# A weighted sum of two experts' outputs: the first tile loaded in one DMA in place of two

## The chip, the cores and the metric

The kernel runs on one core of a Trainium2 chip. The metric is the device time of one execution in microseconds (us), as the median of several runs. The profile is one execution taken by the hardware profiler; its span is a little shorter than the time (237.3 us against 239.03), since it starts with the first instruction.

The engines that matter here are VectorE (called DVE in the profile), ScalarE (ACT), SyncE (SP), and the core's 16 DMA engines, which move data between the chip's main memory (HBM) and the on-chip memory of 128 partitions. DMAs are issued by SyncE and by ScalarE. Each of the two has a DMA queue of its own: q1 is SyncE's, q10 is ScalarE's.

## The reference

For each of 16 x 1024 = 16,384 tokens there are two vectors of 512 floats, one from each of two experts, and two weights. The result is their weighted sum.

```python
def setup_inputs():
    batch, seq, hidden, n_experts, k = 16, 1024, 512, 8, 2
    return {
        "expert_outputs": np.random.randn(batch, seq, k, hidden).astype(np.float32),
        "combine_weights": np.random.randn(batch, seq, k).astype(np.float32),
    }

def reference(expert_outputs, combine_weights):
    weights = combine_weights[..., np.newaxis]
    return np.sum(expert_outputs * weights, axis=2).astype(np.float32)
```

The kernel must read 67.1 MB of vectors and 0.13 MB of weights and write 33.6 MB. There are two products and one addition for every element of the result.

## The kernel before

A token is a row of 1024 floats (4 KB): the 512 of the first expert, then the 512 of the second. Each of the 128 partitions has 128 tokens: 120 in ten tiles of 12 (`J`, g = 0 to 9), and 8 (`LAST`) in a last tile, g = 10. In memory the 120 tokens of one partition lie side by side, so a tile of 12 tokens is one contiguous run of 48 KB in each partition. There are four tile buffers (`bufs=4`).

```python
    J, LAST = 12, 8
    main = per - LAST                      # 120
    ...
    last = main // J                       # 10
    wpool = ctx.enter_context(tc.tile_pool(name="w", bufs=1))
    ipool = ctx.enter_context(tc.tile_pool(name="in", bufs=4))
    wt = wpool.tile([P, per * k], dt)

    for t, c in ((0, main), (main, LAST)):      # weights: rows of 960 B, then of 64 B
        nc.scalar.dma_start(
            out=wt[:, k * t : k * (t + c)].rearrange("p (t k) -> p t k", k=k), in_=cw(t, c)
        )
    ...
    for g in range(last + 1):
        et = ipool.tile([P, J, k * h], dt)
        ot = ...                                # the result, in the front half of et itself
        t0, c = g * J, J if g < last else LAST

        for a, m in ((0, 2), (2, c - 2)) if g == 0 else ((0, c),):
            nc.sync.dma_start(
                out=et[:, a : a + m],
                in_=eo(t0 + a, m),
                max_dma_last_dim=k * h * 4 if g + a == 0 else None,
            )
        if g < last - 1:                        # tiles 0 to 8
            wb = wt[:, g * J * k : (g + 1) * J * k].unsqueeze(2).to_broadcast([P, J * k, h])
            ek = et.rearrange("p j (k h) -> p (j k) h", k=k)
            nc.vector.tensor_tensor(out=ek, in0=ek, in1=wb, op=mult)
            nc.vector.tensor_tensor(out=ot, in0=et[:, :, 0:h], in1=et[:, :, h : 2 * h], op=add)
            nc.scalar.dma_start(out=o(t0, c), in_=ot)
            continue
        ...                                     # tiles 9 and 10: ScalarE takes the first product,
                                                # VectorE the rest
        nc.sync.dma_start(out=o(t0, c), in_=ot[:, 0:c])
```

The weights are loaded in two DMAs from ScalarE's queue: 120 tokens' weights (960 B in each partition) and those of the last tile (64 B). Tile 0 is loaded in two DMAs: tokens 0 and 1, cut into rows of 4 KB by `max_dma_last_dim`, and tokens 2 to 11 in rows of 40 KB. All other tiles of 12 come in one DMA with rows of 48 KB. The first VectorE product of a tile covers all of its 12 tokens and is one instruction. A buffer is loaded anew when its result has been stored.

Of the kernel before, what the change touches and what calls it, by code (L numbers as in the profile page):

```python
# [1 line left out]

# [4 lines left out]


@with_exitstack
def kernel(  # L10
    ctx: ExitStack,
    tc: tile.TileContext,
    expert_outputs: bass.AP,
    combine_weights: bass.AP,
    out: bass.AP,
):

    nc = tc.nc  # L20
    b, s, k, h = expert_outputs.shape
    assert k == 2
    n = b * s
    P = nc.NUM_PARTITIONS
    per = n // P
    assert per * P == n
    J, LAST = 12, 8
    main = per - LAST
    assert main % J == 0
    eo = expert_outputs.rearrange("b s k h -> (b s) (k h)")  # L30
    cw = combine_weights.rearrange("b s k -> (b s) k")
    o = out.rearrange("b s h -> (b s) h")

    def rows(x):

        a = x[0 : P * main, :].rearrange("(p t) f -> p t f", p=P)
        b = x[P * main : n, :].rearrange("(p t) f -> p t f", p=P)
        return lambda t, c: a[:, t : t + c, :] if t < main else b[:, t - main : t - main + c, :]

    eo, cw, o = rows(eo), rows(cw), rows(o)  # L40

    dt = mybir.dt.float32
    mult = mybir.AluOpType.mult
    add = mybir.AluOpType.add
    copy = mybir.ActivationFunctionType.Copy

    last = main // J
# [6 lines that stand above are left out]
    for t, c in ((0, main), (main, LAST)):  # L54
        nc.scalar.dma_start(
            out=wt[:, k * t : k * (t + c)].rearrange("p (t k) -> p t k", k=k), in_=cw(t, c)
        )

    warm = wpool.tile([P, 1], dt)
    nc.scalar.activation(out=warm, in_=nc.const_aps.tensor(1.0, (P, 1), dt), func=copy)  # L60

    for g in range(last + 1):
        et = ipool.tile([P, J, k * h], dt)

        ot = et.rearrange("p j f -> p (j f)")[:, 0 : J * h].rearrange("p (j f) -> p j f", f=h)
        t0, c = g * J, J if g < last else LAST

        for a, m in ((0, 2), (2, c - 2)) if g == 0 else ((0, c),):
            nc.sync.dma_start(  # L69
                out=et[:, a : a + m],  # L70
                in_=eo(t0 + a, m),
                max_dma_last_dim=k * h * 4 if g + a == 0 else None,
            )
        if g < last - 1:

            wb = wt[:, g * J * k : (g + 1) * J * k].unsqueeze(2).to_broadcast([P, J * k, h])
# [7 lines that stand above are left out]
        for i in range(c):  # L84
            t = t0 + i
            nc.scalar.activation(  # L86
                out=et[:, i, 0:h], in_=et[:, i, 0:h], func=copy, scale=wt[:, 2 * t : 2 * t + 1]
            )
            if g == last:
                nc.vector.scalar_tensor_tensor(  # L90
                    out=ot[:, i, :],
                    in0=et[:, i, h : 2 * h],
                    scalar=wt[:, 2 * t + 1 : 2 * t + 2],
                    in1=et[:, i, 0:h],
                    op0=mult,
                    op1=add,
                )
        if g < last:
            w1 = wt.rearrange("p (t k) -> p t k", k=k)[:, t0 : t0 + c, 1:2]
            x1 = et[:, :, h : 2 * h]  # L100
            nc.vector.tensor_tensor(out=x1, in0=x1, in1=w1.to_broadcast([P, c, h]), op=mult)  # L101
            nc.vector.tensor_tensor(out=ot, in0=et[:, :, 0:h], in1=x1, op=add)  # L102
        nc.sync.dma_start(out=o(t0, c), in_=ot[:, 0:c])


# [1 line left out]
_INS = ['expert_outputs', 'combine_weights']  # L107
_OUTS = [((16, 1024, 512), 'float32')]


# [23 lines left out]
```

## Time and profile before

| | before |
|---|---|
| time, median of 3 runs | 239.03 us (238.98 to 239.05) |
| span of the profile | 237.3 us |
| VectorE busy | 193.9 us (82%) |
| ScalarE busy | 14.0 us (6%) |
| moved by DMA | 100.80 MB, 425 GB/s over the span |
| VectorE product of 12 tokens (line L78), mean | 12.96 us |
| VectorE sum of 12 tokens (line L79), mean | 6.56 us |
| a load of 12 tokens, 6144 KB, median from issue to landing | 29.9 us |
| a store of 12 tokens, 3072 KB, median from issue to landing | 32.7 us |

How to read it: the DMA row of the page cuts the span into 40 slices and gives the busy share of the 16 DMA engines in tenths. A line of a DMA queue gives packets, MB, and the time that the packets took as a share of 16 engines' span. A packet here is one contiguous row, or a completion signal of 4 bytes, of which each DMA leaves one on each of the 16 engines. The chain of waits is followed back from the last instruction, at each step to what released it. A line of DMA issues gives the size of one DMA and the time from its issue to the landing of its last byte; that time includes waiting behind other transfers. In a line of the timeline the bracket tells how long the engine stood idle before the instruction, and for what. In a line of the windows stand busy time and number of instructions of DVE, ACT and POOL, the clock of TensorE (not used here), the share of time of the 16 DMA engines by packets that start in the window, and GB/s.

### The profile page before, as it was taken

To read this page: it belongs to the slowest core of one execution; us is meant where nothing else is said; L and a number is where in the kernel's file an instruction comes from. 1 tells how busy PE (TensorE), PEld (TensorE's weight loads), DVE (VectorE), ACT (ScalarE), POOL (GpSimd) and SP (SyncE) were. 2 spreads that over 40 slices of the span, in tenths; PEclk is the share of its full clock that TensorE was granted. 3 is DMA by queue.
4 is the path that set the end of the run, shared out by engine and by line. 5 is a ranking of instruction groups with operands and counts; after the bars stand their busy time and mean duration, and the time that the engine had idled before them with its cause. 6 is when DMAs were issued, how large, how long until landed. Compare 5 with 4: busy or idle time off the path is not lost.

```text
span 237.3 us, 154 instructions
## 1 busy us (share of the span) xinstructions
DVE 193.9 (82%) x28; ACT 14.0 (6%) x22; POOL 0.2 (0%) x4
## 2 busy tenths in 40 slices
DVE  0008999999999999999999879969996998785710
ACT  2000000000000000000000000000000000740800
POOL 0000000000000000000000000000000000000000
DMA  8999999989899999999897999999997979999997
GB/s 308 443 456 406 398 431 497 398 356 505 356 439 435 427 464 464 398 398 522 348 522 344 452 427 435 464 464 398 398 522 340 530 336 460 458 403 442 402 438 309
DMA packets 3728, 100.80 MB, mean 425 GB/s; under 512 B 528, under 2 KB 656, under 8 KB 912
## 3 DMA queue, kind: packets, MB, share of 16 engines
q1 hardware_dynamic: 2144, 72.35, 71.1%
q10 hardware_dynamic: 1584, 28.44, 27.9%
HBM read 67.24 MB, written 33.55 MB: 425 GB/s over the span
## 4 chain that ended last, share of the span: by engine, by line
DMA 59%; DVE 33%; ACT 2%; DVEq 0%; ACTq 0%; issue 0%; SPq 0%
DMA et<-in_expert_outputs_dram 30%; DMA out_dram<-et 29%; DVE et L78 22%; DVE et L79 11%; ACT et L86 2%; DVE et L90 1%; DVEq L129 0%; ACTq L129 0%; SPq L69 0%; DVEq L78 0%; ACTq L86 0%
## 5 line engine op out<-in xcount | busy, mean ns | idle before, releaser
L78 DVE TENSOR_TENSOR et<-et,wt 128x12288 f32<-128x12288 f32 x9 | 116.6, 12955 | 25.2 <-DMA et<-in_expert_outputs_dram 25.2
L79 DVE TENSOR_TENSOR et<-et 128x6144 f32<-128x6144 f32 x9 | 59.0, 6558 | 0.3
L86 ACT ACTIVATE et<-et,wt 128x512 f32<-128x512 f32 x20 | 12.5, 707 | 209.2 <-DMA et<-in_expert_outputs_dram 209.2
L90 DVE SCALAR_TENSOR_TENSOR et<-et,wt 128x512 f32<-128x512 f32 x8 | 5.6, 748 | 3.9 <-ACT et L86 3.7
L101 DVE TENSOR_TENSOR et<-et,wt 128x6144 f32<-128x6144 f32 x1 | 6.6, 6559 | 2.3 <-DMA et<-in_expert_outputs_dram 2.3
L102 DVE TENSOR_TENSOR et<-et 128x6144 f32<-128x6144 f32 x1 | 6.6, 6559 | 0.9 <-ACT et L86 0.9
L60 ACT ACT_TABLE_LOAD x1 | 1.3, 1283 | 1.7 <-issue 1.7
L60 ACT ACTIVATE warm<-const-float32-1.0 128x1 f32<-128x1 f32 x1 | 0.2, 202 | 0.0
L118 POOL MEMSET const-bfloat16-1.0<- 128x1 bf16 x1 | 0.1, 102 | 0.0
L118 POOL MEMSET const-uint8-127<- 128x1 uint8 x1 | 0.1, 102 | 0.0
L118 POOL MEMSET const-float32-0.0<- 128x1 f32 x1 | 0.1, 99 | 0.2 <-issue 0.2
L118 POOL MEMSET const-float32-1.0<- 128x1 f32 x1 | 0.1, 99 | 0.0
## 6 DMA issues: line engine op xcount, KB each, us to landing
et<-in_expert_outputs_dram SPq DMA_DIRECT2D x9, 6144.0 KB, 29.9
out_dram<-et ACTq DMA_DIRECT2D x9, 3072.0 KB, 32.7
et<-in_expert_outputs_dram SPq DMA_DIRECT2D x1, 5120.0 KB, 17.3
et<-in_expert_outputs_dram SPq DMA_DIRECT2D x1, 4096.0 KB, 25.1
out_dram<-et SPq DMA_DIRECT2D x1, 3072.0 KB, 14.6
out_dram<-et SPq DMA_DIRECT2D x1, 2048.0 KB, 10.0
et<-in_expert_outputs_dram SPq DMA_DIRECT2D x1, 1024.0 KB, 5.4
wt<-in_combine_weights_dram ACTq DMA_DIRECT2D x1, 120.0 KB, 4.4
```

The costliest lines, as they stand in the source:

```text
L60: nc.scalar.activation(out=warm, in_=nc.const_aps.tensor(1.0, (P, 1), dt), func=copy)
L78: nc.vector.tensor_tensor(out=ek, in0=ek, in1=wb, op=mult)
L79: nc.vector.tensor_tensor(out=ot, in0=et[:, :, 0:h], in1=et[:, :, h : 2 * h], op=add)
L86: nc.scalar.activation(out=et[:, i, 0:h], in_=et[:, i, 0:h], func=copy, scale=wt[:, 2 * t : 2 * t + 1])
L90: nc.vector.scalar_tensor_tensor(out=ot[:, i, :], in0=et[:, i, h : 2 * h], scalar=wt[:, 2 * t + 1 : 2 * t + 2], in1=et[:, i, 0:h], op0=mul ...
L101: nc.vector.tensor_tensor(out=x1, in0=x1, in1=w1.to_broadcast([P, c, h]), op=mult)
L102: nc.vector.tensor_tensor(out=ot, in0=et[:, :, 0:h], in1=x1, op=add)
L118: nc = _bacc.Bacc("TRN2", target_bir_lowering=False, num_devices=1)
```

## The change

Tile 0 is loaded like all the others: one DMA of 12 tokens in rows of 48 KB. The two DMAs of before, with 256 rows of 4 KB and 128 rows of 40 KB, become one with 128 rows of 48 KB. The purpose is a simpler start, with fewer DMAs and only long rows.

```diff
-        for a, m in ((0, 2), (2, c - 2)) if g == 0 else ((0, c),):
-            nc.sync.dma_start(
-                out=et[:, a : a + m],
-                in_=eo(t0 + a, m),
-                max_dma_last_dim=k * h * 4 if g + a == 0 else None,
-            )
+        nc.sync.dma_start(out=et[:, 0:c], in_=eo(t0, c))
```

## The prediction

> **What bounds the kernel now.** I read the page from the top: busy time of each engine, the DMA row over the span, the DMA queues, then the chain of waits.
>
> ```profile
> span 237.3 us, 154 instructions
> DVE 193.9 (82%) x28; ACT 14.0 (6%) x22; POOL 0.2 (0%) x4
> DMA  8999999989899999999897999999997979999997
> DMA packets 3728, 100.80 MB, mean 425 GB/s; under 512 B 528, under 2 KB 656, under 8 KB 912
> q1 hardware_dynamic: 2144, 72.35, 71.1%
> q10 hardware_dynamic: 1584, 28.44, 27.9%
> DMA 59%; DVE 33%; ACT 2%; DVEq 0%; ACTq 0%; issue 0%; SPq 0%
> ```
>
> VectorE, the busiest engine, has 18% of the span free; the DMA engines have none. The packets of the two queues took 71.1% + 27.9% = 99.0% of 16 engines' span, 234.9 us for each engine. The trace's records of single packets agree: the first data packet starts at 1.81 us, the last ends at 236.18, and I find no gap in between in which an engine stood still for more than 0.15 us. Of the 237.3 us, 1.8 are the start before data moves, 1.1 the end after the last packet, and 234.4 are 16 engines working without a pause (the records overlap by a few ns, so their sum is a little above). The dips to 7 in the DMA row are slices that long packets straddle: a packet is counted where it starts.
>
> The chain of waits names DVE for 33%, but that is a path through a loop (a load needs a free buffer, which needs a store, which needs DVE). As long as either queue has something to move, a delay on that path costs nothing. Its beginning, which the change touches:
>
> ```profile
> 1.22 17.29 DMA et<-in_expert_outputs_dram
> 18.51 0.03 issue
> 18.54 0.05 DVEq L78
> 18.59 0.05 issue
> 18.64 12.97 DVE et L78
> 31.60 0.02 issue
> 31.63 6.56 DVE et L79
> ```
>
> The chain starts at the second DMA, not the first: DVE's first product waits for both halves of tile 0 and for the main weight load. The 1024 KB half arrives 5.4 us after its issue and lies unused until 18.5.
>
> ```profile
> et<-in_expert_outputs_dram SPq DMA_DIRECT2D x1, 5120.0 KB, 17.3
> et<-in_expert_outputs_dram SPq DMA_DIRECT2D x1, 1024.0 KB, 5.4
> wt<-in_combine_weights_dram ACTq DMA_DIRECT2D x1, 120.0 KB, 4.4
> wt<-in_combine_weights_dram ACTq DMA_DIRECT2D x1, 8.0 KB, 17.1
> ```
>
> Look at the last two: the 8 KB of weights need 17.1 us to land and the 120 KB only 4.4. Both are 128 short rows, 8 on each DMA engine. The difference is what stands in the other queue: 4 KB rows in the first case, 40 KB rows in the second.
>
> **What the Trainium skill says.** "DMA: Bandwidth & Descriptors", section "Queues, rings and completion order", says that each DMA engine goes round-robin between its queues, a whole packet at a time. The trace agrees: behind the short rows each engine's records alternate, one 40960-byte packet (1.514 us), one 64-byte packet (0.011 us), and eight such rounds, 8 x 1.52 = 12.2 us, are the bulk of those 17.1. The same page's section "Issuing engines are not separate DMA queues" says that transfers from different queues share the same 16 engines; so a saturated kernel cannot gain by order alone, and the 99.0% above says this one is saturated. Under "Where 436 GB/s comes from" the page gives a ceiling of 435 GB/s; the mean here is 425, and a long packet's rate is 49152 B / 1.815 us x 16 = 433 GB/s.
>
> **The change part by part.** On every engine the compute instructions and their order stay the same; one DMA issue leaves SyncE. Per DMA engine:
>
> 1. Packets removed: 16 of 4096 B (128 partitions x 2 tokens, 256 in all) at a steady 0.159 us = 2.54 us; 8 of 40960 B at 1.514 = 12.11; one completion packet, 0.01. Together 14.67.
> 2. Packets added: 8 of 49152 B at 1.815 (median of the 1152 there now) = 14.52 us. Saved: 14.67 - 14.52 = **0.15 us**, all of it on the saturated resource.
> 3. The ramp. The 256 short packets took 3.21 us per engine in sum, 0.67 more than 16 x 0.159: the first ones last 0.2 to 1.0 us each. The windows of 1 us show it (the last two numbers are DMA share and GB/s):
>
> ```profile
> 1.00:2.00 1.00, 0.00 (x0) 0.26 (x1) 0.00 (x0) 1.00 0.40 61
> 2.00:3.00 1.00, 0.00 (x0) 1.00 (x1) 0.00 (x0) 1.00 0.77 182
> 3.00:4.00 1.00, 0.00 (x0) 0.22 (x2) 0.00 (x0) 1.00 1.00 371
> 4.00:5.00 1.00, 0.00 (x0) 0.00 (x0) 0.00 (x0) 1.00 1.08 430
> ```
>
> With 48 KB rows some of this excess may vanish, if it is paid per packet, or none, if it belongs to the first moments of reading. I book 0 to 0.4 us saved, middle 0.1.
>
> 4. The weights come later. Now 8 rows of 960 B (0.044 us each) slip between 4 KB rows. After the change each waits for a 48 KB row. In the records of before most engines start with two packets of the load queue, then alternate strictly. Carried over: rows 1 and 2, weight row 1, row 3, weight row 2, and so on to row 8, weight row 7, tile 0's completion, weight row 8, the first row of tile 1, the weights' completion. So I expect the 120 KB to land one long packet, 1.8 us, behind tile 0. Tile 0's data end at about 1.9 (mean first packet) + 14.52 + 7 x 0.044 + a ramp of 0.3 to 0.7 = 17.0 to 17.4 us; some 0.6 us more to landing and 1.8 for the weights puts DVE's first product at 19.5 to 20.2, say **19.9 instead of 18.6**. The 8 KB of weights follow eight or more rounds later, at 35 to 39; only the last tile reads them, past 200 us.
> 5. Does the 1.3 us matter? DVE runs tiles 0 to 5 back to back, 12.95 + 6.56 us each (the pair's period is 19.46), until 135.5 and then waits:
>
> ```profile
> 137.66 12.96 DVE L78 TENSOR_TENSOR et<-et,wt 128x12288 f32<-128x12288 f32 x1 [2.17 <-DMA et<-in_expert_outputs_dram]
> 159.43 12.96 DVE L78 TENSOR_TENSOR et<-et,wt 128x12288 f32<-128x12288 f32 x1 [2.21 <-DMA et<-in_expert_outputs_dram]
> ```
>
> So DVE catches up at tile 6 at the latest. What a late DVE can do earlier is send out the first store late: 39.5 instead of 38.2 us. The store queue then starts about one long packet later, and the load queue gets one packet ahead. The engines stay busy, since the loads of tiles 1 to 3 are queued until 72 us (the longest load lands 69.3 us after issue), and the fifth load, which waits for the first store, is issued at 64.15: 8 us in hand. At the end, the last store is issued at 226.5 and by the packet records the store ahead of it on the same queue moves until 231.2. With the 1.1 us from issue to first packet there are 3.6 us in hand. Neither margin is used up by 1.3 us, or by 1.8.
>
> Sum: -0.15 (packets) - 0.1 (ramp) + 0 (late weights) = -0.25 us, so **238.8 us**.
>
> **The rivals.** *The late weights reach the end.* If the 1.3 to 1.8 us of DVE were on the path all the way, the time would be 240.3 to 240.8, and with two long packets of delay 242.6. For it: the chain's first third is DVE back to back behind that wait. Against: the 99.0%, DVE's waits of 2.2 us at tiles 6 to 8, the margins of 8 and 3.6 us. Even this is at most 1.5%.
>
> *The ramp goes away.* If all 0.67 us of the short rows' excess is due to their being short, the time is 239.03 - 0.15 - 0.67 = 238.2. For it: the excess sits in the first one to three short packets of each engine. Against: at 39 to 42 us, just when the first store is on its way (issued at 38.22), load packets of 48 KB last up to 2.42 us in place of 1.815, a loss of some 0.6 us per engine; the first use of a direction seems to cost as much with long rows.
>
> *The ramp grows.* Long rows could bind an engine longer to a slow first access; 0.3 us more would give 239.2.
>
> **Range and chances.** The three runs of before lie within 0.07 us, and the sum's terms are fractions of a microsecond, so the range holds the ramp either way and a little of a late tail: 238.2 to 239.5. A change of 2% is 4.8 us, more than the rivals make, two of them together included. Faster 0.01, same 0.98, slower 0.01.
>
> **What would show it right or wrong.** Right: q1 has 272 packets less (256 + 128 rows removed, 128 added, 16 completions less: 2144 - 272 = 1872); the two shares still sum to 99%; the 120 KB of weights land at 18 to 20 us after issue, the one 6144 KB load of tile 0 at about 17; DVE starts at 19.5 to 20.2; its wait at tile 6 shrinks from 2.17 us to under 1. If DVE starts at 18 us, step 4 (two load packets before the first weight row) is wrong. If the packets' shares fall below 98%, step 5 is wrong and there is idle DMA time to be found, first about 64 to 72 us or after 226. If the 1 us windows show the ramp reaching 430 GB/s at another time, step 3 is what was mis-sized.

## The result: 0.3% slower at the median, and scattered

The changed kernel takes 239.80 us at the median of 6 runs (239.11, 239.14, 239.72, 239.88, 240.15, 240.50). The kernel before takes 238.99 (238.93 to 239.05). The ratio is 1.0031, with a 95% interval of 1.0016 to 1.0046. That is within the 2% that was forecast as near certain, but outside the forecast range of 238.2 to 239.5, and of the other sign than the forecast gain of 0.25 us. The scatter is the first thing to notice: 0.12 us before, 1.4 us after. A part of the difference is luck. All six runs of the kernel before were quick, but beside the experiments below 27% of its runs (81 of 299) were not; at that share six quick ones in a row are an estimated one case in seven. By the means of the larger sets below, the change costs 0.2 to 0.3 us (239.59 against 239.41, and 239.65 against 239.38).

The page of the changed kernel, from its top, in the profiled run (239.88 us):

```profile
span 238.1 us, 154 instructions
DVE 194.0 (81%) x28; ACT 14.0 (6%) x22; POOL 0.2 (0%) x4
DMA  7999999999999999999999999899999999999995
DMA packets 3456, 100.80 MB, mean 423 GB/s; under 512 B 512, under 2 KB 640, under 8 KB 640
q1 hardware_dynamic: 1872, 72.35, 70.8%
q10 hardware_dynamic: 1584, 28.44, 27.8%
```

The 272 packets fewer on q1 are there. The two shares sum to 98.6% of 238.1 us, 234.8 us for each engine, against 234.9 before. So the DMA engines have no more to do, yet the span is 0.8 us longer. The dips of before are gone from the DMA row: packets no longer start in lockstep on all engines. The last slice fell from 7 to 5.

The lines of the DMA issues and the start of the chain of waits:

```profile
et<-in_expert_outputs_dram SPq DMA_DIRECT2D x10, 6144.0 KB, 31.6
wt<-in_combine_weights_dram ACTq DMA_DIRECT2D x1, 120.0 KB, 17.7
wt<-in_combine_weights_dram ACTq DMA_DIRECT2D x1, 8.0 KB, 31.8
```

```profile
0.72 17.67 DMA wt<-in_combine_weights_dram
18.39 0.02 issue
18.41 12.97 DVE et L73
```

The weights now land last, as foreseen, but at 18.39, hardly behind tile 0. DVE starts at 18.41, 0.23 us earlier than before. A late start of DVE is not the cause. DVE's wait at tile 6 did not shrink to under 1 us either: it is 2.29 us, and a new one of 1.70 us stands at tile 5.

```profile
117.51 12.96 DVE L73 TENSOR_TENSOR et<-et,wt 128x12288 f32<-128x12288 f32 x1 [1.70 <-DMA et<-in_expert_outputs_dram]
139.35 12.96 DVE L73 TENSOR_TENSOR et<-et,wt 128x12288 f32<-128x12288 f32 x1 [2.29 <-DMA et<-in_expert_outputs_dram]
```

The loads come late: a load takes 31.6 us from issue to landing at the median, 1.7 us more than before, almost one 48 KB packet.

### Where the time is: one DMA engine out of sixteen

The windows of 1 us around the first store, and the one at the end, of the changed kernel (DMA share and GB/s are the last two numbers; a window counts the packets that start in it):

```profile
41.00:42.00 1.00, 1.00 (x1) 0.00 (x0) 0.00 (x0) 1.00 1.99 713
42.00:43.00 1.00, 1.00 (x1) 0.00 (x0) 0.00 (x0) 1.00 0.17 49
43.00:44.00 1.00, 1.00 (x1) 0.00 (x0) 0.00 (x0) 1.00 0.98 418
236.00:237.00 1.00, 0.00 (x0) 0.00 (x0) 0.00 (x0) 1.00 0.04 16
```

The same windows of the kernel before:

```profile
41.00:42.00 1.00, 1.00 (x1) 0.00 (x0) 0.00 (x0) 1.00 2.18 737
42.00:43.00 1.00, 1.00 (x1) 0.00 (x0) 0.00 (x0) 1.00 0.00 0
43.00:44.00 1.00, 1.00 (x1) 0.00 (x0) 0.00 (x0) 1.00 0.91 393
236.00:237.00 1.00, 0.00 (x0) 0.00 (x0) 0.00 (x0) 1.00 0.00 0
```

A number of GB/s in a window of 1 us is kilobytes. Before: 393 is 16 x 24.576, so all 16 engines start their first store row in 43 to 44, and none starts anything in 42 to 43. After: 713 is 14 x 49.152 + 24.576, so one engine has begun its first store row before 42, and the 49 in the next window are its next load row alone. And at the end, one 16 KB row of the last store starts after 236.0, by itself; before, none does.

The trace has each DMA packet's start and duration but not its engine. I joined the packets to 16 chains by end and start. For the changed kernel (us; "extra" is the duration above the median of packets of that size):

```
                     first packet  first store row  extra at 36-48 us  end
the engine in question   1.86          41.88             1.26          236.96
the other fifteen     1.75-2.63     43.08-43.80       0.20-0.68     235.67-236.20
kernel before, all 16 1.81-2.10     43.26-43.78       0.60 (mean)   235.72-236.18
```

The engine that takes the store first pays for it: its load packet before the store lasts 2.24 us and the one after 2.65, in place of 1.815. On the other fifteen these two last 1.97 to 2.38 and 1.81 to 2.03 us, so the difference is in the one after. Every DMA is divided evenly over the engines, 8 rows to each: every one of the 16 chains, the late one too, has 80 load rows of 48 KB and 80 store rows of 24 KB. So nobody takes over what one engine has lost; it stays behind to the end, 0.77 us after the next one, and the span ends with it.

### The profile page after: what moved, and what is told of

It is laid out like the page before. It is cut to its first block, busy times and chain, and to the rows that moved or that the text cites. A ratio compares the mean times of both kernels' runs of the same rounds, so it can differ in the third digit from the quotient of the medians.

```text
span 238.1 us, 154 instructions
## 1 busy us (share of the span) xinstructions
DVE 194.0 (81%) x28; ACT 14.0 (6%) x22; POOL 0.2 (0%) x4
## 4 chain that ended last, share of the span: by engine, by line
DMA 60%; DVE 33%; ACT 2%; DVEq 0%; ACTq 0%; issue 0%; SPq 0%
DMA out_dram<-et 28%; DMA et<-in_expert_outputs_dram 25%; DVE et L73 22%; DVE et L74 11%; DMA wt<-in_combine_weights_dram 7%; ACT et L81 2%; DVE et L85 1%; DVEq L124 0%; ACTq L124 0%; SPq L68 0%; DVEq L73 0%; ACTq L81 0%
## 6 DMA issues: line engine op xcount, KB each, us to landing
et<-in_expert_outputs_dram SPq DMA_DIRECT2D x10, 6144.0 KB, 31.6
```

## The experiments

The theory to test (theory 1): the first store reaches the 16 engines close to their packet boundaries. Depending on a tenth of a microsecond, one or more engines take it one 48 KB packet earlier than the rest. Those out of step lose 0.5 to 1 us there, and the slowest engine sets the end. The rivals: the long first rows make the start uneven (theory 2), and late weights or later work of VectorE (theory 3). Runs fall into two groups, 238.9 to 239.4 and 239.5 to 241.3 us, with only 12 of the 641 runs between; I count those at 239.5 and above as the upper group. The groups are clear in the two kernels themselves, less so in some variants. The experiments ran on several chips, each beside many runs of the kernel before.

**a_again** is the changed kernel as it is.

> The changed kernel once more, for the spread of its times and a second profile. Theory 1 (one or a few of the 16 DMA engines take the first store's first packet one 48 KB packet earlier than the others, lose some 0.8 us there, and the end is set by the slowest engine): times spread over 239.1 to 240.5 us again, median about 239.7; in a slow profile one engine's first store packet starts near 41.9 us and the others' near 43.1 to 43.8. Theory 2 (the long first rows make the start itself uneven: an engine that begins late stays late): the same spread, but the engine that ends last is one whose first packet started last.

Measured: 239.76 median of 14, 8 of them in the upper group; the kernel before beside it 239.10, with 21 of 67 in the upper group. The ratio is 1.0007 (0.9991 to 1.0023), so this set alone doesn't tell the two kernels apart. So **the kernel before has the same trouble on this chip, only less often**; its first six runs had shown none. The profile (239.78 us) again has one engine with its first store row at 41.75 and 15 at 43.32 to 43.72; that engine ends at 236.86, the others at 235.73 to 236.11. Its first data packet started before 2.06 like all others, so theory 2 in its simple form (who starts last ends last) fails.

**a_tap**: the first store a little later.

```diff
+            if g == 0:
+                nc.scalar.activation(out=ot[:, 0, 0:1], in_=ot[:, 0, 0:1], func=copy)
             nc.scalar.dma_start(out=o(t0, c), in_=ot)
```

> The changed kernel with a ScalarE copy of one column of tile 0's result onto itself ahead of the first store, which sends the first store out some 0.3 us later and touches nothing else. Theory 1: all 16 engines are again on the same side, no engine takes the store early, median 238.9 to 239.1 us with a spread under 0.2 us, as before. Theory 2, and theory 3 (the late weights or the later work of VectorE cost the time): no gain, 239.5 to 240.0 with the spread of the changed kernel.

Measured: 239.06 median of 22, all between 238.92 and 239.26, none in the upper group. Its ratio to the kernel before is 0.9985 (0.9974 to 0.9996). Two lines of its timeline, one of its DMA issues and three of its windows:

```profile
38.09 0.20 ACT L76 ACTIVATE et<-et 128x1 f32<-128x1 f32 x1 [34.94 <-DVE et L74]
38.32 0.35 ACTq L77 DMA_DIRECT2D out_dram<-et  x1
```

```profile
et<-in_expert_outputs_dram SPq DMA_DIRECT2D x10, 6144.0 KB, 29.9
```

```profile
42.00:43.00 1.00, 1.00 (x1) 0.00 (x0) 0.00 (x0) 1.00 0.00 0
43.00:44.00 1.00, 1.00 (x1) 0.00 (x0) 0.00 (x0) 1.00 0.91 393
236.00:237.00 1.00, 0.00 (x0) 0.00 (x0) 0.00 (x0) 1.00 0.00 0
```

An added instruction and a store 0.24 us later make the kernel quicker: all 16 engines are in step again, and a load takes 29.9 us as in the kernel before. Loads, weights and start are those of the changed kernel, so theory 3 falls, and theory 2 as the cause of the upper group.

**b_early10 and b_early18**: the kernel before, its first store earlier. Tile 0's product leaves out the last 10 (18) of 512 columns, which stay unweighted; all else is done.

```diff
-            nc.vector.tensor_tensor(out=ek, in0=ek, in1=wb, op=mult)
+            z = h - 10 if g == 0 else h
+            nc.vector.tensor_tensor(out=ek[:, :, 0:z], in0=ek[:, :, 0:z], in1=wb[:, :, 0:z], op=mult)
```

> The kernel before, with the product of tile 0 leaving out 10 of 512 columns, so that its first store goes out 0.25 us earlier; the loads stay as they were, the 4 KB rows included. Theory 1: the engines with the latest packet boundaries now take the store one packet early, 239.4 to 240.5 us and a spread of 0.5 us or more. Theories 2 and 3: 239.0 us, as before.

> As the last, but 18 of 512 columns left out, 0.45 us earlier. Theory 1: about five of the 16 engines take the store early; 239.4 to 240.5 us. Theories 2 and 3: 239.0 us.

Measured: 239.84 (239.51 to 240.28, 22 of 22 in the upper group) and 239.65 (20 of 22). Less work and an earlier store make the kernel before as slow as the changed one, with the short rows in place. In the profile of b_early18:

```profile
41.00:42.00 1.00, 1.00 (x1) 0.00 (x0) 0.00 (x0) 1.00 1.24 467
42.00:43.00 1.00, 1.00 (x1) 0.00 (x0) 0.00 (x0) 1.00 1.43 442
43.00:44.00 1.00, 1.00 (x1) 0.00 (x0) 0.00 (x0) 1.00 0.40 172
```

442 is 9 load rows and 172 is 7 store rows: nine engines took the store in 41 to 42, seven after 43. I had expected five early ones. And here not only a few engines lose time: the extra is 1.00 to 1.26 us on the nine early ones and 0.90 to 0.98 us on the seven others. In b_early10 two engines were early, and ended at 237.0 and 237.3.

**b_tap, b_early36, a_dve, a_touch** came next, on another chip. b_tap is a_tap's copy in the kernel before; b_early36 leaves out 36 columns.

> The kernel before with the same ScalarE copy of one column ahead of its first store, some 0.3 us of delay. Theory 1: no engine takes the store early, every run between 238.9 and 239.3 us, also on a chip on which some runs of the kernel before lie at 239.8 and above. Against a_tap (239.06) it shows what the short first rows themselves are worth once the first store is out of the matter: I expect 0.0 to 0.2 us in favour of the long rows, so 239.0 to 239.2 here.

Measured: 239.09 median of 12, 2 in the upper group (239.50 and 239.92), against 25 of 63 of the unaltered kernel before beside it. The delay helps there too, but not in every run as expected. The gain of the long rows over this (239.06 against 239.09) is 0.03 us, too little to count, as the two ran on different chips.

> The kernel before, with the product of tile 0 leaving out 36 of 512 columns: the first store goes out 0.9 us earlier. Theory 1: now all or nearly all 16 engines take the store one packet early, together, first store packets near 41 to 42 us on all; with all in step again the time goes back to 238.9 to 239.3 us although the store is earlier than in b_early10 and b_early18. If instead an early store is costly in itself, 239.6 or more.

Measured: 239.79, 17 of 20 in the upper group. This went against the expectation, though the profile (239.69) still has two groups: 14 engines take the store at 41.5 to 41.8, while two load packets last 3.3 us and are followed by another load. With all but two early, it is the two that are out of step; but the other fourteen lose time as well, 0.95 us at the mean, where 0.60 are lost in the profile of the kernel before.

a_dve delays the store by a VectorE instruction of 0.15 us:

```diff
             nc.vector.tensor_tensor(out=ek, in0=ek, in1=wb, op=mult)
+            if g == 0:
+                nc.vector.tensor_copy(out=et[:, 0, 0:1], in_=et[:, 0, 0:1])
```

> The changed kernel with one more tiny VectorE instruction (a copy of one column onto itself) between product and sum of tile 0, about 0.1 us of delay of the first store, to measure how narrow the margin is. Theory 1: the distance from the store's issue to the last engine's packet boundary falls from 1.65 to about 1.55 us, between that of the changed kernel and the 1.46 of the kernel before: runs at 239.7 and above become fewer than half of all, median 239.0 to 239.3. If the delay does nothing: median 239.7.

Measured: 239.01 median of 20, all between 238.91 and 239.25, none in the upper group; 0.9978 (0.9966 to 0.9990) of the kernel before. The expectation was too cautious: 0.19 us is enough. All 16 first store rows start at 43.20 to 43.65.

a_touch asks why the load packets at 39 to 44 us are long in all kernels (its edit, abridged):

```diff
+    nc.scalar.dma_start(out=o(0, 1)[:, 0, 0:1], in_=warm)     # before all stores
-    for t, c in ((0, main), (main, LAST)):                    # the 64 B rows: SyncE, with tile 6
```

> The changed kernel with a store of 4 bytes per partition (the constant 1.0) to the output's first column, issued at the start and overwritten later by tile 0's result, which waits for it; the last tile's weights are loaded later, by SyncE. It tests where the 0.5 us that each engine loses at 39 to 44 us come from. If they are paid once for the first writing of the output's places in memory, load packets of 1.815 us stay so at 39 to 44 us and the time falls to 238.4 to 238.7, whichever side the engines fall on. If they belong to turning from reading alone to reading and writing, the long packets stay and the time is 239.0 to 240.

Measured: 239.54, 10 of 20 in the upper group. The extra is still there, 0.65 us per engine at the mean. A first write of 4 bytes in each partition's part of the output doesn't take it away. The profiled run (239.42) has all engines in step, and its last one ends at 236.50 with 0.75 us extra; so a part of a run's time can also come without anyone being out of step.

**a_third, a_tap1536, b_early46, a_dve2**, on a third chip: is it the place between packet boundaries, or just "too early"?

> The changed kernel a third time, as the measure for the other three on the same chip. Runs at 239.0 to 239.4 us where all engines are in step, at 239.7 to 240.5 where one or more are not, median 239.4 to 239.9.

Measured: 239.93, 13 of 21 in the upper group, ratio 1.0015 (1.0003 to 1.0028). The profiled run happened to be a quick one, 238.99, and has all 16 first store rows at 43.19 to 43.67. So the same kernel shows both pictures, with the times that go with them.

> The changed kernel with the ScalarE copy of a_tap made longer, 1536 columns, so that the first store goes out some 1.76 us later in place of 0.24: nearly one 48 KB packet (1.815 us). If what counts is where the store falls between packet boundaries (theory 1), the distance from the issue to the last engine's boundary is again about 1.7 us and single engines take the store one packet ahead of the others: median 239.6 to 240.0, first store packets in two groups near 43.5 and 45 us. If what counts is only that the store is not too early, it is as quick as a_tap: 239.0 to 239.1.

The edit is that of a_tap with `ot[:, 0:3, :]`. Measured: 239.76, 19 of 21 in the upper group; the store is issued at 39.53, 1.5 us later than without the copy (I had expected 1.76), and the kernel is slow again. Windows of its profile (239.32):

```profile
43.00:44.00 1.00, 1.00 (x1) 0.00 (x0) 0.00 (x0) 1.00 1.32 516
44.00:45.00 1.00, 1.00 (x1) 0.00 (x0) 0.00 (x0) 1.00 1.27 442
45.00:46.00 1.00, 1.00 (x1) 0.00 (x0) 0.00 (x0) 1.00 0.40 172
```

172 in 45 to 46 are seven engines' first store rows, the 516 before hold nine (9 x 24.576 + 6 x 49.152): two groups, one packet later than in b_early18. By the median, late is as bad as early; so the place counts.

> The kernel before with 46 of 512 columns left out of tile 0's product: the first store some 1.15 us earlier, 0.25 more than in b_early36, where 14 of 16 engines took it early. If all 16 now take it together, theory 1 says 238.9 to 239.2 us. If an early store costs time by itself, 239.6 or more, no quicker than b_early36 (239.79).

Measured: 239.76, 9 of 13 in the upper group, so the median missed. Yet the profiled run, at 238.95, is the in-step case that I was after:

```profile
41.00:42.00 1.00, 1.00 (x1) 0.00 (x0) 0.00 (x0) 1.00 0.91 393
42.00:43.00 1.00, 1.00 (x1) 0.00 (x0) 0.00 (x0) 1.00 1.82 786
236.00:237.00 1.00, 0.00 (x0) 0.00 (x0) 0.00 (x0) 1.00 0.00 0
```

All 16 stores start in 41 to 42, a packet earlier than in the kernel before, and nothing is lost. So an early store need not cost anything; why most of the other runs were slow, this profile can't show.

> The changed kernel with the tiny VectorE copy (0.19 us of delay of the first store), on another chip if it falls so. As a_dve: all runs between 238.9 and 239.3 us, median 239.0, quicker in the mean than both kernels wherever the kernel before has runs at 239.8 and above.

Measured: 239.02 median of 21 (238.86 to 239.37), none in the upper group, where the kernel before had 19 of 65. The interval of the ratio, 0.9982 to 1.0000, just reaches 1.

**a_tap768, split_8k, w_first, b_early46b** were for what was still open.

> The changed kernel with the ScalarE copy at 768 columns, a delay of the first store of about 0.9 us, halfway between a_tap (0.24 us, quick) and a_tap1536 (1.5 us, slow). If the place between packet boundaries decides, this is the middle of the safe stretch: every run 238.9 to 239.3 us, all 16 first store packets within 0.7 us of each other. If a longer delay costs by itself, 239.3 to 239.6.

The copy covers `ot[:, 0:3, 0:256]`. Measured: 239.13, 2 of 20 in the upper group; store issued at 38.91. That is the safe stretch between two unsafe ones, though not free of exceptions.

> The kernel before without the cut into 4 KB rows: tile 0 still in two DMAs, 2 tokens in rows of 8 KB and 10 in rows of 40 KB. The weights land early, as before. If the late landing of the weights is what moved the odds, this behaves like the kernel before: most runs at 239.0 to 239.3, a third or fewer at 239.7 and above, median 239.0 to 239.2. If the 4 KB rows themselves kept the engines in step, it behaves like the changed kernel: more than half at 239.7 and above, median 239.5 to 239.9.

The edit removes the line `max_dma_last_dim=...` from the kernel before. Measured: 238.98 median of 12, 2 in the upper group: like the kernel before (13 of 63 there). The 4 KB rows are not what kept it in step.

```diff
-        nc.scalar.dma_start(
+        (nc.sync if t == 0 else nc.scalar).dma_start(
             out=wt[:, k * t : k * (t + c)].rearrange("p (t k) -> p t k", k=k), in_=cw(t, c)
         )
```

> The changed kernel with the main weight load issued by SyncE ahead of tile 0, so that one DMA with 48 KB rows loads tile 0 and the weights still land early; VectorE waits for the tile last, as in the kernel before. If the late landing of the weights moved the odds: like the kernel before, median 239.0 to 239.3, a third or fewer of the runs at 239.7 and above. If the long first rows did it: like the changed kernel, median 239.5 to 239.9. The 0.35 us that the weights take ahead of tile 0 are moved in any case and cost nothing.

Measured: 240.12, 16 of 20 in the upper group, the slowest of all. The weights land after 2.1 us and it didn't help: an early landing of the weights doesn't bring the odds of before back. One engine is again alone:

```profile
42.00:43.00 1.00, 1.00 (x1) 0.00 (x0) 0.00 (x0) 1.00 0.24 74
43.00:44.00 1.00, 1.00 (x1) 0.00 (x0) 0.00 (x0) 1.00 0.74 319
236.00:237.00 1.00, 0.00 (x0) 0.00 (x0) 0.00 (x0) 1.00 0.08 33
```

74 is one store row and one load row in a window in which the kernel before starts nothing.

> b_early46 once more, for a second profile. If the profiled run is a slow one (239.6 us or more), theory 1 expects one to four engines whose first store packet comes two to three us after the others', as in b_early36; if it is slow with all 16 first store packets within 0.7 us of each other, theory 1 does not explain it and an early store has a cost of its own.

Measured: 239.45, 10 of 20 in the upper group. The profiled run was a quick one (238.98) and has all engines in step at 41.42 to 41.80. It couldn't decide the question.

**a_wt2late and w_first_dve** end the series. a_wt2late loads the 64-byte weight rows with tile 6, so that none stand between the rows of tile 1; w_first_dve is w_first with a_dve's copy.

```diff
-    for t, c in ((0, main), (main, LAST)):
+    for t, c in ((0, main),):
...
+        if g == 6:
+            nc.sync.dma_start(out=wt[:, k * main :].rearrange("p (t k) -> p t k", k=k), in_=cw(main, LAST))
```

> The changed kernel with the 8 KB of the last tile's weights loaded much later, by SyncE, so that no short rows stand between the rows of tile 1. If these rows moved the odds, the last engine's boundary comes 0.06 us nearer to the store's issue (1.58 to 1.60 us in place of 1.64 to 1.68) and a third of the runs or fewer are at 239.5 and above, median 239.0 to 239.2, like the kernel before. If not: more than half, median 239.6 or more, like the changed kernel.

> w_first (240.12 us) with the tiny VectorE copy of a_dve, 0.19 us of delay of the first store. If its slowness is one engine out of step (distance 1.72 us in its profile, 1.53 after the delay): nearly all runs at 239.0 to 239.4. If early weights ahead of tile 0 cost time in another way, 239.8 or more.

Measured: a_wt2late 239.25, 3 of 21 in the upper group (kernel before beside it: 239.07, 3 of 41), so the share is 14% where the changed kernel had about 60%. But the changed kernel itself was not run in this set, and the kernel before was at 7% here, against 31% and 21% in two earlier sets on the same chip; so that supports the reading and doesn't prove it; and its lower group lies 0.12 us above that of the kernel before (239.18 against 239.06). w_first_dve 239.41 (from 240.12), 8 of 21 still in the upper group. Most of w_first's loss is the missed step, but not all: its profile (239.49) has every engine in step, and yet the engines end at 235.95 to 236.46, where those of a_dve end at 235.64 to 236.04. Tile 0's rows end within 0.63 us of each other, no further apart than in a_again (0.64). So what is left is not an uneven start: all engines are late, by 0.36 us at the mean. Part of it stands at the start, where the packets' extra is 0.95 us per engine against 0.77 in a_dve.

### What decides the step

For each engine, take the first load row that starts after the store has been issued. The latest of these sixteen starts, less the time of the issue, is the distance. It is worked out to the nanosecond from the joined chains; b_early18 and a_tap1536, with many engines on each side, are left out:

```
kernel, time of the profiled run     store issued   latest engine's   distance   engines out
                                                    load row starts              of step
b_early36     239.69                    36.83           37.50           0.67        2
a_tap768      239.08                    38.91           39.69           0.78        0
b_early46b    238.98                    36.79           37.76           0.96        0
b_early46     238.95                    36.64           37.63           0.98        0
a_tap         238.95                    38.32           39.65           1.33        0
b_tap         239.13                    38.22           39.60           1.38        0
a_dve         238.99                    38.20           39.64           1.44        0
a_dve2        239.07                    38.17           39.62           1.45        0
before                                  38.22           39.68           1.46        0
w_first_dve   239.49                    38.38           39.92           1.54        0
a_wt2late     239.18                    38.15           39.73           1.58        0
a_touch       239.42                    38.04           39.67           1.63        0
split_8k      239.15                    37.95           39.59           1.63        0
after         239.88                    37.99           39.64           1.645       1
a_third       238.99                    37.98           39.62           1.646       0
a_again       239.78                    38.00           39.68           1.69        1
b_early10     240.23                    37.77           39.47           1.70        2
w_first       240.26                    38.33           40.05           1.72        1
```

But for b_early36, no engine is out of step up to 1.63 us, and one or two are from 1.69 us on; between, at 1.645 and 1.646, the changed kernel shows both. An engine whose load row starts later than that takes the store right behind this row; an earlier one takes one more load row first.

What sets the distance? VectorE waits for the last row of tile 0 (in the changed kernel, of the weights) on the latest engine, and the store follows 19.6 us after VectorE's start. From the end of that last row to the row boundary in question it is 21.77 us in the kernel before and 21.82 in the changed one, because on every engine eight 64-byte rows now stand behind the first rows of tile 1, where they had been among tile 0's. From the end of the same row to VectorE's start it is 0.73 us in the profile of before and 0.59 in that of after. So of the 0.18 us between their distances (1.46 and 1.645), only 0.05 come from the order of rows. The rest is this delay, which differs from profile to profile: 0.55 to 0.76 us in all kernels but w_first and w_first_dve. That the profile of before stands at 1.46 is an accident too: b_tap without its 0.24 us would be at 1.62, and split_8k is at 1.63.

So both kernels stand near the edge, the changed one on it. The 0.05 us, with a_wt2late, are the likeliest explanation of the odds (8 of 14 and 13 of 21 runs of the changed kernel in the upper group, against 21 of 67 and 19 of 65 of the kernel before beside them); they are supported, not settled. w_first, which is worse without such rows, doesn't speak against them: there VectorE starts only 0.45 us after the last row, and that alone puts the latest engine at 1.72. Why the delay is shorter there, no run shows.

Step and time go together, though not perfectly. The seven profiles with engines out of step took 239.32 to 240.26 us, the twelve with all in step whose time is on record 238.95 to 239.49.

## Why the prediction was wrong, point by point

- **The bound.** Right that the DMA engines are saturated, and that the sum of their packets would stay: 234.9 to 234.8 us. Wrong in what followed from it. "16 engines working without a pause" is a sum over engines; the span ends with the slowest one. The sum's small fall in packets was right and the time rose, since one engine ended 0.77 us after the rest. Nor does it hold that a saturated kernel "cannot gain by order alone": a_dve moves the same data with the first store 0.19 us later, and gains.
- **Steps 1 and 2**, 0.15 us saved on packets, hold as arithmetic on the records. **Step 3**, the ramp, was mis-sized and of the wrong sign: extra per engine in the first packets is 0.66 us before and 0.77 after (0.77 to 0.91 in the other profiles that start in the same way). So steps 1 to 3 sum to -0.04 to +0.10 in place of -0.25. The rival "the ramp grows" was nearer. The runs agree: of the lower group alone, the medians are 239.04 to 239.09 for the changed kernel and 239.05 to 239.07 for the one before. The windows of the changed kernel's start:

```profile
1.00:2.00 1.00, 0.00 (x0) 0.35 (x1) 0.00 (x0) 1.00 1.70 492
2.00:3.00 1.00, 0.00 (x0) 0.99 (x2) 0.00 (x0) 1.00 0.87 295
3.00:4.00 1.00, 0.00 (x0) 0.14 (x1) 0.00 (x0) 1.00 0.00 0
4.00:5.00 1.00, 0.00 (x0) 0.00 (x0) 0.00 (x0) 1.00 1.88 802
```

  Ten engines start within the first window and six in the second; their next rows, with one shared round of weights, come at 4.4. All 16 first rows are long, 2.0 to 3.0 us; of the next 16 only one is (2.04).
- **Step 4**, DVE at 19.9, was wrong. The first weight row stands behind one load row, not behind two (in the changed kernel the earliest weight row starts at 4.34 us, the earliest second load row at 4.38), and the weights land with tile 0: DVE started at 18.41. From there on the two queues alternate row by row, long rows and short. The two short rows ahead of the weights in the records of before were probably the 0.4 us by which the first weight rows came later (2.19 against 1.81 us), not a fixed number of rows. The sum was off as well: 17.0 to 17.4 with 0.6 and 1.8 is 19.4 to 19.8, not 19.5 to 20.2. The data of tile 0 ended at 17.30 to 17.78 us, a little later than foreseen.
- **Step 5**, that the place of the first store is free as long as both queues have work, is the step that failed. The step asked only whether some queue has work, and that held: in the changed kernel no DMA engine stands still between 3 and 235 us, so the margins of 8 and 3.6 us were not used up. What it counted as free, the place of the first store, cost one engine 1.26 us where the others lost 0.20 to 0.68; that engine set the end. What I had not considered is that the store can change the order of packets on some engines and not on others, and that an engine alone in its order loses more at the first exchange of loads and stores. The profile before had it in view: I quoted load packets of 2.42 us at 39 to 42 us for the ramp and didn't ask what happens to an engine that meets them at another moment.
- **The range** rested on three runs within 0.07 us. Beside the experiments the same kernel had 27% of its runs at 239.5 us and above. The quick runs of the changed kernel (239.11 and 239.14) lie inside the range.
- "Within 2%" held. The rival of late weights was not put to the test, since VectorE did not start late; what cost the time is in none of the three rivals.

## What to carry to other kernels

When DMA engines are saturated and every transfer is divided evenly over them, compare the engines with each other: the time is the slowest one's, and a sum or a share of all 16 can't show it. If a time scatters in two groups, look for an event that falls close to a boundary, and move it by a tenth of a microsecond either way: here one tiny VectorE instruction (0.15 us, all 41 runs of two chips at 238.86 to 239.37) did more than the change of the load, and beats both kernels in the mean: 239.04 and 239.08 us against 239.52 and 239.38 of the kernel before beside it, and 239.65 of the changed kernel beside the second.

## What was unexpected of the hardware, and what stays open

- A store issued 1.646 us before a load row's start did not come right behind that row: one more load row went first (a_third). The first packets of the kernel start 1.0 us after the first issue (0.72 to 1.75 us), so a part of this may be the way from the issue to the engines; how the 1.65 us divide, no run shows. In b_early10, b_early18 and a_tap1536, where many engines are near the limit, some at 1.68 to 1.86 us take one more load row too, and in a_tap1536 some at 1.59 to 1.63 don't; so the limit differs by engine.
- At the first exchange of loads and stores each engine loses 0.4 to 0.65 us at the mean of the in-step profiles, once; later exchanges show next to nothing. An engine alone in its order loses up to 1.3, and in b_early18 and b_early36 all sixteen lose 0.7 to 1.6. Why, no run shows; a_touch only excludes that the first write of 4 bytes per partition settles it.
- The place isn't the whole rule. b_early36 (0.67 us) stands where a_tap768 stands (0.78), yet 17 of 20 of its runs were in the upper group against 2 of 20, and two of its engines kept to loads although by the limit all 16 should have taken the store. Half or more of the runs of b_early46 and its repetition (0.98 and 0.96 us) were in the upper group too, of which none was profiled. Their quick runs show that an early store need not be costly; what separates the others is open.
- w_first is slower than all, partly because all its engines end later (by 0.36 us in w_first_dve). Only a part of that is seen at the start, and what causes it was not tried.
